# Hybrid decoder layer on one core: an own tile for a temporary of the early FFN products, two tiles for the third weight block of the joint FFN, and the final scalings spread over later passes

## The chip, the core and the metric

The kernel runs on one core of a Trainium2 chip. Five engines work side by side, each through its own list of instructions in order: PE (TensorE) multiplies matrices into PSUM, DVE (VectorE) and ACT (ScalarE) do elementwise work, POOL (GpSimd) does some elementwise work and issues transfers, SP (SyncE) issues most transfers between DRAM and SBUF. An instruction waits on semaphores that other engines or landed transfers raise; what stands behind it on its engine waits too.

The metric is the device time of one execution in microseconds (us).

## The reference

One layer: RWKV-7 time mixing and an indexer-selected sparse attention side by side, merged by gates, then a dense SwiGLU FFN and a last RMSNorm. 1024 tokens, width 1024, all in float32. The change touches the end of the merge, the FFN and the last norm:

```python
z = rmsnorm(h, norm2_g)                   # h: the layer's sum after the merge
g, u = split(z @ w_ffn_in, 2)             # D_FF = 2816
h = h + (silu(g) * u) @ w_ffn_out
out = rmsnorm(h, normf_g)
```

This is the core of it, written out in short.

## The kernel before

**Number format.** Every float32 operand x is split into a high part (ACT, L116) and the rest (DVE, L117: `lo = x - hi`), and a product is three matmuls for each 128 rows: hi·hi, hi·lo, lo·hi (`mm3`, L146, L147, L151). A matmul is 128 x 128 times 128 x 512.

**Tiling.** Everything stands transposed: 128 channels on the partitions, tokens along the row. The tokens are two halves of 512 (`HT`). The FFN's inner width is 22 blocks of 128 (`NFF`). Blocks 0 to 7 (`EARLY`) are done for each half apart; blocks 8 to 21 are done for both halves jointly in four groups (`JOINT`: 4, 3, 3 and 4 blocks), each followed by its part of the output product.

**Buffers.** Results of products go to PSUM: `acc` (three banks) and `mix` (five). `tmp()` gives the next of four [128, 512] tiles in SBUF; whoever takes one waits until its last user, often a store to DRAM, is done. Raw weights land in `wst` (three tiles), their parts in `whi`/`wlo` (two each).

**Order.** PE's list is written out by hand: generators yield counts of matmuls, and `fill`, `pump` and `tiles` slip FFN products of half 0 between the attention's products of half 1. The lists of the other engines follow from the order in which the program issues their instructions, with those under `high_priority` moved ahead.

**Early products.** While the attention of half 1 runs, `ahead(j, zs)` (L1327) computes for j = 8 to 21 two products p and x of half 0 with half a weight tile each, scales them by a row (L1335, L1337), adds them (L1338), forms silu(x) in t (`silu`, L1317 on ACT, L1318 on DVE) and stores p and t to `d_p[j]` (L1336, L1340). p, x and t are three `tmp()`. Just before it, `ffn_out` for half 0 adds blocks 0 to 7 to the sum in `d_h`: load into a `tmp()`, add (L1362), store (L1363).

**Merge and sums.** `merge(1, ...)` (L1183) multiplies the gates into the outputs of half 1 (L1199, L1213), with `mid` for the first half of the sum. `combined` (L1446) loads the stored z of half 0 (`d_z`, L1461), scales it into one of two `t` tiles (L1462) and builds the sums t1, t2 and t4 of both halves' activations.

**Joint tile.** For one block j, `joint_in` (L1505) needs five sums of products in place of six: two with `wb` (acc and mix, L1527 and L1530), the third with the first half of `wc` (L1533), the fourth with `wd` (L1535), and the fifth with the second half of `wc`, added in PSUM to the third (L1538). So the fifth may start only when L1533 has read the third. `sums` (L1480) forms the weight combinations on POOL (four operations, L1444); `blocks` (L1492) splits them into `wb`, `wc`, `wd`. Both are issued one tile ahead. In the groups, tiles 8, 9, 10, 12, 13, 15, 16, 18, 19, 20 prepare the next one's blocks; the first of a group gets its blocks from the output product of the group before.

**End.** `finish_out` (L1393) does the output product of the last group in three passes: half 0, the first 256 tokens of half 1, and the last 256. In each it adds eight products to h (L1425) and sums the squares (`Rms.add`, L259 on ACT, L260 on DVE). `norm_out` (L1383) then scales the eight rows (L1390) and stores them; it runs in the middle of the next pass, all eight rows at once.

Of the kernel before, what the change touches and what calls it, by code (L numbers as in the profile page):

```python
# [50 lines left out]
def block_kernel(ctx: ExitStack, tc: tile.TileContext, ins: dict, outT: bass.AP, stop=None, dbg=None):  # L51
# [1131 lines left out]
    def merge(half, zp, zs, jp=None):  # L1183
# [7 lines left out]
        if half:  # L1191
            mid = jp.tile([128, 8, HT], F32, tag="t3", name="mid")
            for d in range(8):
                w = weights(ins["w_o"][d][:, 0:4, :], 4)
                ga = tmp()
                SY.dma_start(ga, d_g[half][d])
                pa = acc()
                yield from mm3(pa, w, yt, nk=4)
                V.scalar_tensor_tensor(mid[:, d, :], ga, 1.0, pa, op0=ALU.add, op1=ALU.mult)  # L1199
# [5 lines left out]
        for d in range(8):  # L1205
            if half:
# [5 lines left out]
                ga = mid[:, d, :]  # L1212
# [113 lines left out]

    def ahead(j, zs):  # L1327
# [6 lines left out]
        p, x, t = tmp(), tmp(), tmp()  # L1334
# [7 lines left out]
    def ffn_out(f, g0, gn, halves, ring=None, raw=None, last=None):  # L1342
# [16 lines left out]
        def add(d, half, ps):  # L1359
            t = tmp() if ring is None else ring[:, (2 * d + half) % 8, :]  # L1360
# [22 lines left out]
    def norm_out(half, sq):  # L1383
# [4 lines left out]
        for k in range(8):  # L1388
            u = sq.h[:, k, sq.tok]
            V.scalar_tensor_tensor(u, u, par[:, P_NF + k:P_NF + k + 1], rb, op0=ALU.mult, op1=ALU.mult)  # L1390
            SY.dma_start(outT[k * 128:(k + 1) * 128, half * HT + sq.tok.start:half * HT + sq.tok.stop], u)

    def finish_out(zps, jp, f, g0, gn):  # L1393

        whi, wlo = (zps[0].tile([128, 8, gn, 128], F32R, tag=t, name=n) for t, n in (("s1", "fhi"), ("s3", "flo")))
        hs = [jp.tile([128, 8, HT], F32, tag="t3", name="h"), zps[1].tile([128, 8, HT], F32, tag="s1", name="h")]
        ws, before = [], None
        for half in range(2):
            for d in range(8):
                G.dma_start(hs[half][:, d, :], d_h[half][d])  # L1400
# [7 lines left out]
        for half, tok in ((0, slice(0, HT)), (1, slice(0, 256)), (1, slice(256, HT))):  # L1408
# [8 lines left out]
            for d in range(8):  # L1417
# [7 lines left out]
                V.tensor_tensor(h[:, d, tok], h[:, d, tok], ps, op=ALU.add)  # L1425
# [79 lines left out]
    def joint_in(f, gn, i, j, bs, ring, jp):  # L1505

        wb, wc, wd = prepared.pop(j)
        p1, t0, w, c = (ring[:, j % 2, e, :] for e in range(4))
        SY.dma_start(ring[:, j % 2, 0:2, :], d_p[j])
# [22 lines left out]
        with urgent():  # L1532
            V.tensor_tensor(c, w, pc, op=ALU.add)  # L1533
# [106 lines left out]
    if fill:  # L1640
        tiles(1)
    sb.close()
    (sz1, zp1), z1 = opened("right", "zp1"), []
    with tc.tile_pool(name="jp", bufs=1, side="right", reuse_waits="tile") as jp:
        run_over(merge(1, zp1, z1, jp))
# [15 lines left out]
        more = jp.tile([128, 8, HT], F32, tag="t3", name="more")  # L1661
        ring = zp1.tile([128, 2, 4, HT], F32, tag="s0", name="ring")
# [5 lines left out]
        finish_out(both, jp, f, *JOINT[-1])  # L1668
# [81 lines left out]
```

## Time and profile before

| What | us |
|---|---|
| Median of 3 runs (1744.35 to 1752.37) | 1746.75 |
| Profiled execution | 1742.06 |
| Its span | 1740.3 |
| PE busy | 1681.8 |
| DVE busy | 1178.5 |
| ACT busy | 823.6 |
| POOL busy | 177.2 |
| Span without PE's busy time (worked out) | 58.5 |

A row of a timeline gives start, duration, engine, line, operation, what it writes and reads, and in brackets how long the engine had been idle and what released it. "DVE tmp L1335" is the DVE instruction of line 1335 that writes `tmp`. A q behind an engine's name is its queue, which issues transfers. The idle time of PE stands in a few places: the start, the early products, the attention's softmax, the merge, the joint tiles and the last passes.

### The profile page before, as it was taken

What the parts mean: (1) busy time and instruction counts of PE and PEld (TensorE: products, weight loads), DVE (VectorE), ACT (ScalarE), POOL (GpSimd) and SP (SyncE); (2) the same over time, 40 slices, a digit from 0 to 9 for tenths busy, and PEclk for the clock granted to TensorE, in tenths of its full rate; (3) what the DMA queues carried; (4) which work ended last, traced back from release to release, by engine and by line L of the source; (5) the groups of instructions that cost most, each with busy time, mean ns of one, the idle gap of its engine ahead of it and who ended that gap; (6) DMA issues with size and microseconds to landing.
All of it is one profiled execution on the core that took longest, in us unless ns stands there. A gap on an engine that the chain in (4) does not pass through costs nothing.

```text
span 1740.3 us, 26809 instructions
## 1 busy us (share of the span) xinstructions
PE 1681.8 (97%) x9952; PEld 1382.1 (79%) x9952; DVE 1178.5 (68%) x2277; ACT 823.6 (47%) x1585; POOL 177.2 (10%) x179
## 2 busy tenths in 40 slices
PE   8999999999999999999999899999999999999997
PEld 6888888788877777877787688878788878787777
DVE  6789989857578457956885465674874463746566
ACT  6365998553444688645324266533442231322231
POOL 0000000010021111000100221000000321221320
PEclk9999999999999999999999899999999999999998
DMA  5542224536265524664342774476445446475532
GB/s 211 164 145 95 100 98 146 163 102 176 89 192 172 161 89 155 203 192 148 103 131 95 226 205 132 154 235 198 145 129 186 139 134 223 138 229 185 170 108 97
DMA packets 149090, 268.13 MB, mean 154 GB/s; under 512 B 38704, under 2 KB 63984, under 8 KB 148832
## 3 DMA queue, kind: packets, MB, share of 16 engines
q1 hardware_dynamic: 125600, 192.59, 34.5%
q10 hardware_dynamic: 15552, 47.75, 8.7%
q0 software_dynamic: 7808, 26.09, 5.5%
q8 instruction: 78, 1.28, 0.3%
q14 instruction: 52, 0.43, 0.1%
HBM read 195.54 MB, written 70.83 MB: 153 GB/s over the span
## 4 chain that ended last, share of the span: by engine, by line
PE 61%; DVE 9%; DMA 4%; ACT 3%; issue 2%; POOL 2%; SPq 0%; POOLq 0%; DVEq 0%; ACTq 0%
PE acc L146 14%; PE acc L151 13%; PE acc L147 13%; DVE wlo L117 2%; PE mix L1093 2%; PE mix L1518 2%; PE acc L161 2%; PE mix L1069 2%; PE mix L1522 2%; PE mix L1520 2%; PE mix L1083 2%; DMA wst<-in_w_ffn_in 1%; DMA d_h<-tmp 1%; PE mix L828 1%; PE mix L840 1%
## 5 line engine op out<-in xcount | busy, mean ns | idle before, releaser
L117 DVE TENSOR_TENSOR wlo<-wst,whi 128x1024 fp32r<-128x1024 f32 (+1 forms) x177 | 210.1, 1189 | 159.2 <-ACT whi L116 89.6
L116 ACT ACTIVATE whi<-wst 128x1024 fp32r<-128x1024 f32 (+1 forms) x177 | 173.9, 984 | 221.3 <-PE acc L147 147.9
L146 PE MATMUL acc<-zhi,whi 128*128 128x512 f32 x336 | 133.7, 398 | 7.8 <-DVE tmp L1335 7.4
L146 PE MATMUL acc<-u1hi,whi 128*128 128x512 f32 x352 | 140.3, 398 | 0.0
L147 PE MATMUL acc<-u1lo,whi 128*128 128x512 f32 x352 | 138.1, 392 | 0.0
L146 PE MATMUL acc<-u0hi,whi 128*128 128x512 f32 (+1 forms) x352 | 135.3, 387 | 1.8 <-DVE tmp L352 1.8
L147 PE MATMUL acc<-u0lo,whi 128*128 128x512 f32 (+1 forms) x352 | 133.8, 383 | 0.0
L147 PE MATMUL acc<-zlo,whi 128*128 128x512 f32 x336 | 132.1, 393 | 0.0
L146 PE MATMUL acc<-fhi,whi 128*128 128x512 f32 x236 | 92.8, 393 | 1.0 <-ACT whi L116 1.0
L147 PE MATMUL acc<-flo,whi 128*128 128x512 f32 x236 | 92.1, 390 | 1.0 <-DVE flo L117 1.0
L151 PE MATMUL acc<-u1hi,wlo 128*128 128x512 f32 x352 | 90.4, 396 | 0.0
L151 PE MATMUL acc<-zhi,wlo 128*128 128x512 f32 x336 | 87.2, 395 | 0.0
L151 PE MATMUL acc<-u0hi,wlo 128*128 128x512 f32 (+1 forms) x352 | 86.6, 385 | 0.0
L146 PEld LDWEIGHTS acc<-zhi,whi 128*128 128x128 f32 x336 | 63.7, 190 | 22.2 <-DVE tmp L1335 7.8
L146 PEld LDWEIGHTS acc<-u1hi,whi 128*128 128x128 f32 x352 | 67.1, 191 | 14.7 <-DVE tmp L343 0.4
L146 PEld LDWEIGHTS acc<-u0hi,whi 128*128 128x128 f32 x352 | 66.2, 188 | 15.2 <-ACT stg L116 2.2
L147 PEld LDWEIGHTS acc<-u1lo,whi 128*128 128x128 f32 x352 | 66.8, 190 | 13.3
L151 PEld LDWEIGHTS acc<-u1hi,wlo 128*128 128x128 f32 x352 | 65.7, 189 | 14.4 <-issue 1.2
L147 PEld LDWEIGHTS acc<-u0lo,whi 128*128 128x128 f32 x352 | 66.2, 188 | 12.2
L151 PEld LDWEIGHTS acc<-u0hi,wlo 128*128 128x128 f32 x352 | 64.0, 188 | 13.1 <-issue 0.7
L147 PEld LDWEIGHTS acc<-zlo,whi 128*128 128x128 f32 x336 | 63.7, 190 | 12.5
L151 PEld LDWEIGHTS acc<-zhi,wlo 128*128 128x128 f32 x336 | 62.9, 189 | 13.2 <-issue 0.3
(421 smaller groups left out, 3945.3 us busy)
## 6 DMA issues: line engine op xcount, KB each, us to landing
wst<-in_w_ffn_in SPq DMA_DIRECT2D x58, 512.0 KB, 3.6
wst<-in_w_in ACTq DMA_DIRECT2D x36, 512.0 KB, 3.4
wst<-in_w_in SPq DMA_DIRECT2D x27, 512.0 KB, 3.5
k<-d_k POOLq DMA_DIRECT2D x24, 512.0 KB, 7.5
more<-d_h SPq DMA_DIRECT2D x48, 256.0 KB, 4.3
d_h<-more SPq DMA_DIRECT2D x48, 256.0 KB, 3.8
h<-in_xT SPq DMA_DIRECT2D x32, 256.0 KB, 5.0
d_g<-tmp ACTq DMA_DIRECT2D x32, 256.0 KB, 2.5
```

The costliest lines, as they stand in the source:

```text
L116: A.activation(hi, x, AF.Copy)
L117: V.tensor_tensor(lo, x, hi.bitcast(F32), op=ALU.subtract)
L146: T.matmul(ps, whi[:, wk + k, :], ahi[:, ak + k, tok], start=k == 0, stop=False)
L147: T.matmul(ps, whi[:, wk + k, :], alo[:, ak + k, tok], start=False, stop=False)
L151: T.matmul(ps, wlo[:, wk + k, :], ahi[:, ak + k, tok], start=False, stop=k == nk - 1)
L161: T.matmul(ps, w[:, k, :], a[:, k, tok], start=k == 0 and w is whi and a is ahi, stop=k == nk - 1 and a is alo)
L1069: T.matmul(ps[:, :w], q[bi // 2][:, e, bi % 2 * 128:bi % 2 * 128 + 128], k[:, i, e, c:c + w], start=i == 0, stop=i == 1)
L1083: T.transpose(ps[:, j * 128:(j + 1) * 128], L[:, (c + j) * 128:(c + j + 1) * 128], ident)
L1093: T.matmul(py[64 * e:64 * e + 64, bi * 128:(bi + 1) * 128], v[:, j, 64 * e:64 * e + 64], pts[e][j // 4][:, j % 4, :], start=j == b, stop=j ...
L1518: T.matmul(ps, w[0][:, o + k, :], bhi[:, k, :], start=first_ and k == 0, stop=False, skip_group_check=not first_)
L1520: T.matmul(ps, w[0][:, o + k, :], blo[:, k, :], start=False, stop=False, skip_group_check=not first_)
L1522: T.matmul(ps, w[1][:, o + k, :], bhi[:, k, :], start=False, stop=k == 3, skip_group_check=not first_)
```

## The change

Three edits, and what they bring along:

1. **`spare`.** In `ahead`, x gets a tile of its own in place of a `tmp()`: one buffer while the attention runs, and in the merge one of the two `t` buffers that `combined` uses too. p and t stay `tmp()`.
2. **Third weight block.** `wc` is one tile for both parts, and its two buffers alternate (tag "wc", and the room of half of `mid`). `blocks(j + 1)` is issued behind the third addition of tile j, no longer at the tile's start. The tile's sums w and c are `tmp()`, which makes the ring smaller; `mid` and `more` are cut in two.
3. **Rows of the end.** `norm_out` hands back control after each row, and the later pass calls it once for each d. Half 0's h is in the tiles of `more`.

```diff
-            mid = jp.tile([128, 8, HT], F32, tag="t3", name="mid")
+            mid = [jp.tile([128, 4, HT], F32, tag=f"m{i}", name="mid") for i in range(2)]
...
+    spare = [tmp]
...
-        p, x, t = tmp(), tmp(), tmp()
+        p, x, t = tmp(), spare[0](), tmp()
...
             V.scalar_tensor_tensor(u, u, par[:, P_NF + k:P_NF + k + 1], rb, op0=ALU.mult, op1=ALU.mult)
             SY.dma_start(outT[k * 128:(k + 1) * 128, half * HT + sq.tok.start:half * HT + sq.tok.stop], u)
+            yield 0
...
-                if before is not None and d in (1, 3):
-                    next(before, None)
-                    if d == 3:
-                        run(before)
-            before = norm_out(half, sq)
-            next(before)
-        run(before)
+                if len(late) > 1:
+                    next(late[0], None)
+                if late and (d == 1 or d > 2):
+                    next(late[-1], None)
+            if len(late) > 1:
+                run(late.pop(0))
+            late.append(norm_out(half, sq))
+            next(late[-1])
+        for before in late:
+            run(before)
...
-            wc = [jp.tile([128, 8, 128], F32R, tag=t, name=t) for t in ("wchi", "wclo")]
+            wc = jp.tile([128, 2, 8, 128], F32R, tag="m1" if j % 2 else "wc", name="wc")
+            wc = [wc[:, 0], wc[:, 1]]
...
-        p1, t0, w, c = (ring[:, j % 2, e, :] for e in range(4))
+        p1, t0 = (ring[:, 2 * (j % 2) + e, :] for e in range(2))
+        w, c = tmp(), tmp()
...
-            if i + 1 < gn:
-                blocks(j + 1, jp)
...
-            V.tensor_tensor(c, w, pc, op=ALU.add)
+            third = V.tensor_tensor(c, w, pc, op=ALU.add)
+        if i + 1 < gn:
+            with tc.issue_after(third.ins):
+                blocks(j + 1, jp)
...
     with tc.tile_pool(name="at1", bufs=1, side="right", reuse_waits="tile") as ap:
+        spare[0] = lambda: ap.tile([128, HT], F32, tag="spare", name="spare")
...
+        spare[0] = lambda: jp.tile([128, HT], F32, tag="t", name="t", bufs=2)
...
-        more = jp.tile([128, 8, HT], F32, tag="t3", name="more")
-        ring = zp1.tile([128, 2, 4, HT], F32, tag="s0", name="ring")
+        ring = zp1.tile([128, 8, HT], F32, tag="s0", name="ring")
+        more = jp.tile([128, 4, HT], F32, tag="m0", name="more")
+        more = [more[:, i, :] for i in range(4)] + [ring[:, i, :] for i in range(4, 8)]
```

PE's list is the same in both kernels but for the names of the tiles. The other engines' lists change in three places that matter here. Line numbers behind the edits grow by 1 to 11 in the changed kernel (L1335 is L1338 there, L1533 is L1541, L1390 is L1393, L1425 is L1430).

First, the early products on DVE, blocks 8 to 10, where the attention of half 1 begins. The order stays; the waits don't. DMAHW1 is the landing of the d_h store that the profile shows issued at 976.70 us, DMAHW6 that of the one at 971.83 us, DMAHW2 that of block 8's p. Before:

```order
L1335 TENSOR_TENSOR tmp<-acc,row 128x512 [waits DMAHW1_49,PE_49]
L1318 SCALAR_TENSOR_TENSOR tmp<-tmp 128x512 [waits DMAHW6_49,Activation_49]
L1337 TENSOR_TENSOR tmp<-acc,row 128x512 [waits DMAHW2_49,PE_49]
L117 TENSOR_TENSOR wlo<-wst,whi 128x1024 [waits DMAHW5_49,Activation_49]
L1338 TENSOR_TENSOR tmp<-tmp 128x512 [waits DVE_49]
L1335 TENSOR_TENSOR tmp<-acc,row 128x512 [waits DMAHW5_49,PE_49]
L1318 SCALAR_TENSOR_TENSOR tmp<-tmp 128x512 [waits Activation_49]
```

And changed:

```order
L1338 TENSOR_TENSOR tmp<-acc,row 128x512 [waits DMAHW6_49,PE_49]
L1319 SCALAR_TENSOR_TENSOR tmp<-tmp,spare 128x512 [waits DMAHW4_49,Activation_49]
L1340 TENSOR_TENSOR spare<-acc,row 128x512 [waits DVE_49,PE_49]
L117 TENSOR_TENSOR wlo<-wst,whi 128x1024 [waits DMAHW5_49,Activation_49]
L1341 TENSOR_TENSOR spare<-spare,tmp 128x512 [waits DVE_49]
L1338 TENSOR_TENSOR tmp<-acc,row 128x512 [waits DMAHW2_49,PE_49]
L1319 SCALAR_TENSOR_TENSOR tmp<-tmp,spare 128x512 [waits DMAHW1_49,Activation_49]
```

The wait for DMAHW1 has moved from block 9's p to its t, five instructions later; x (L1340) waits for no transfer.

Second, one joint tile on DVE, from the first addition (L1527) to the fourth (L1535), in the last group. Before, the next tile's weights stand ahead of the second and third additions:

```order
L1527 TENSOR_TENSOR ring<-ring,acc 128x512
L117 TENSOR_TENSOR wlo<-wst,whi 128x512
L117 TENSOR_TENSOR wlo<-s_14946,whi 128x512
L1539 SCALAR_TENSOR_TENSOR ring<-ring 128x512
L1530 TENSOR_TENSOR ring<-ring,mix 128x512
L117 TENSOR_TENSOR flo<-ring,fhi 128x512
L1533 TENSOR_TENSOR ring<-ring,mix 128x512
L117 TENSOR_TENSOR wdlo<-wst,wdhi 128x512
L1535 TENSOR_TENSOR ring<-ring,mix 128x512
```

Changed (the names are the same, `wc` holds both parts of the third block):

```order
L1535 TENSOR_TENSOR ring<-ring,acc 128x512
L117 TENSOR_TENSOR flo<-ring,fhi 128x512
L1538 TENSOR_TENSOR tmp<-ring,mix 128x512
L1541 TENSOR_TENSOR tmp<-tmp,mix 128x512
L117 TENSOR_TENSOR wlo<-wst,whi 128x512
L117 TENSOR_TENSOR wlo<-s_14959,whi 128x512
L117 TENSOR_TENSOR wc<-wst,wc 128x1024
L117 TENSOR_TENSOR wdlo<-wst,wdhi 128x512
L1546 TENSOR_TENSOR tmp<-tmp,mix 128x512
```

The four subtractions of the weights have moved behind the third addition (L1541). The subtraction `flo<-ring,fhi`, which belongs to the tile before, stands ahead of it in both; its high part `fhi` stands on ACT behind that of `wst` in both.

Third, the second pass of the end on DVE. Before, all eight scalings of half 0 stand in a row:

```order
L1425 TENSOR_TENSOR h<-h,acc 128x256
L260 TENSOR_TENSOR sacc<-sacc,tmp 128x256
L1390 SCALAR_TENSOR_TENSOR h<-h,par,mix 128x512 x8
L1425 TENSOR_TENSOR h<-h,acc 128x256 x3
L260 TENSOR_TENSOR sacc<-sacc,tmp 128x256 x2
```

Changed:

```order
L1430 TENSOR_TENSOR h<-h,acc 128x256
L261 TENSOR_TENSOR sacc<-sacc,tmp 128x256
L1393 SCALAR_TENSOR_TENSOR more<-more,par,mix 128x512 x2
L1430 TENSOR_TENSOR h<-h,acc 128x256
L1393 SCALAR_TENSOR_TENSOR more<-more,par,mix 128x512
L261 TENSOR_TENSOR sacc<-sacc,tmp 128x256
L1430 TENSOR_TENSOR h<-h,acc 128x256
L1393 SCALAR_TENSOR_TENSOR more<-more,par,mix 128x512
L261 TENSOR_TENSOR sacc<-sacc,tmp 128x256
```

Two scalings stand together, then one for each addition. In the merge, one more effect of the `t` buffers: the first two scalings of `d_z` (L1462), which stood between the merge's first gate products, now stand with the other six behind it, and their loads with them.

More of the change, by code (lines that the diff above doesn't have):

```diff
@@ L245, in __init__ @@
         def __init__(self, h, tok=slice(0, HT)):
-            self.h, self.tok, self.n = h, tok, (tok.stop - tok.start) // 128
+            self.h = h if callable(h) else lambda k: h[:, k, :]
+            self.tok, self.n = tok, (tok.stop - tok.start) // 128
             self.acc = tp.tile([128, HT], F32, tag="sacc", name="sacc", bufs=2)
@@ L1198, in merge @@
                 yield from mm3(pa, w, yt, nk=4)
-                V.scalar_tensor_tensor(mid[:, d, :], ga, 1.0, pa, op0=ALU.add, op1=ALU.mult)
+                V.scalar_tensor_tensor(mid[d // 4][:, d % 4, :], ga, 1.0, pa, op0=ALU.add, op1=ALU.mult)
         for j in range(4, 8):
@@ L1211, in merge @@
                 yield from mm3(pb, w, yt, nk=4, ak=4)
-                ga = mid[:, d, :]
+                ga = mid[d // 4][:, d % 4, :]
                 V.scalar_tensor_tensor(gb, gb, 1.0, pb, op0=ALU.add, op1=ALU.mult)
@@ L1359, in add @@
         def add(d, half, ps):
-            t = tmp() if ring is None else ring[:, (2 * d + half) % 8, :]
+            t = tmp() if ring is None else ring[(2 * d + half) % 8]
             SY.dma_start(t, d_h[half][d])
@@ L1388, in norm_out, with finish_out @@
         for k in range(8):
-            u = sq.h[:, k, sq.tok]
+            u = sq.h(k)[:, sq.tok]
             V.scalar_tensor_tensor(u, u, par[:, P_NF + k:P_NF + k + 1], rb, op0=ALU.mult, op1=ALU.mult)
             SY.dma_start(outT[k * 128:(k + 1) * 128, half * HT + sq.tok.start:half * HT + sq.tok.stop], u)
-    def finish_out(zps, jp, f, g0, gn):
+            yield 0
+    def finish_out(zps, more, f, g0, gn):
         whi, wlo = (zps[0].tile([128, 8, gn, 128], F32R, tag=t, name=n) for t, n in (("s1", "fhi"), ("s3", "flo")))
-        hs = [jp.tile([128, 8, HT], F32, tag="t3", name="h"), zps[1].tile([128, 8, HT], F32, tag="s1", name="h")]
-        ws, before = [], None
+        h1 = zps[1].tile([128, 8, HT], F32, tag="s1", name="h")
+        hs = [lambda k: more[k], lambda k: h1[:, k, :]]
+        ws, late = [], []
         for half in range(2):
             for d in range(8):
-                G.dma_start(hs[half][:, d, :], d_h[half][d])
+                G.dma_start(hs[half](d), d_h[half][d])
         def w(d):
@@ L1507, in joint_in @@
         wb, wc, wd = prepared.pop(j)
-        p1, t0, w, c = (ring[:, j % 2, e, :] for e in range(4))
-        SY.dma_start(ring[:, j % 2, 0:2, :], d_p[j])
+        p1, t0 = (ring[:, 2 * (j % 2) + e, :] for e in range(2))
+        w, c = tmp(), tmp()
+        SY.dma_start(ring[:, 2 * (j % 2):2 * (j % 2) + 2, :], d_p[j])
         if j + 1 < NFF:
             sums(j + 1, jp)
-            if i + 1 < gn:
-                blocks(j + 1, jp)
         def mm(ps, w, o, b, first_=True):
@@ L1639, in block_kernel @@
             pump(abs(n))
-    if fill:
-        tiles(1)
+        if fill:
+            tiles(1)
     sb.close()
@@ L1667, in block_kernel @@
                 run(*ffn_out(f, g0, gn, [0, 1], more, jp, lambda: blocks(g0 + gn, jp)))
-        finish_out(both, jp, f, *JOINT[-1])
+        finish_out(both, more, f, *JOINT[-1])
     sz1.close()
```

8 lines of the change are left out of this document (4 added, 4 removed).

## The prediction

> **What bounds the kernel now.** I read the page's busy times first, then the waits of PE, and then the timelines of PE and of the engine that each large wait names. All times are microseconds from the span's start.
>
> ```profile
> PE 1681.8 (97%) x9952; PEld 1382.1 (79%) x9952; DVE 1178.5 (68%) x2277; ACT 823.6 (47%) x1585; POOL 177.2 (10%) x179
> ...
> PE acc L146 <- DVE tmp L1335: 7.4, 1, 7.4
> PE mix L1518 <- DVE ring L1533: 7.2, 6, 2.7
> PE acc L146 <- DVE mid L1199: 2.7, 1, 2.7
> PE acc L146 <- DVE h L1425: 1.9, 1, 1.9
> ```
>
> The first row is the busy time of each engine; the others are what PE waited for, with total, number of times and longest. PE is busy for 1681.8 of 1740.3, so it is the bound, and the order and number of its matmuls are the same in both kernels. Only PE's idle time can go, 58.5 in all, and the change touches four causes that hold 7.4 + 7.2 + 2.7 + 1.9 = 19.2 of it. I look for the end of each wait in its own stretch. The change is thus worth about 1% at most before anything is lost, and half of that is about what a measurement of this kernel can tell from no change (0.5% is 8.7 us).
>
> **1. The own tile of the early products.** The rows are those of PE, DVE, ACT and SP's queue, and the window (sum, PE, PEld, DVE, ACT, POOL, then the granted clock, the DMA share and GB/s).
>
> ```profile
> 995.74 0.79 PE L146 MATMUL acc<-zhi,whi 128*128 128x512 f32 x1 [7.39 <-DVE tmp L1335]
> 1000.92 0.39 PE L146 MATMUL acc<-zhi,whi 128*128 128x512 f32 x1
> 1006.46 0.77 PE L1083 MATMUL mix<-kc,L 128*128 128x128 f32 x5 [0.75 <-ACT L L1074]
> ...
> 995.00 0.69 DVE L1335 TENSOR_TENSOR tmp<-acc,row 128x512 f32<-128x512 f32 x1 [12.34 <-DMA d_h<-tmp]
> 1003.46 0.48 DVE L1071 CUSTOM_DVE_ANT_0 L<-mix,bias 128x320 f32<-128x320 f32 x1
> ...
> 985.16 0.63 ACT L1317 ACTIVATE tmp<-tmp 128x512 f32<-128x512 f32 x1 [4.78 <-DMA d_h<-tmp]
> ...
> 971.83 0.32 SPq L1363 DMA_DIRECT2D d_h<-tmp  x1
> 976.70 0.32 SPq L1363 DMA_DIRECT2D d_h<-tmp  x1
> 978.23 0.32 SPq L1336 DMA_DIRECT2D d_p<-tmp  x1
> ...
> 987.00:1007.00 20.00, 11.86 (x48) 9.34 (x47) 10.46 (x21) 3.24 (x5) 0.70 (x2) 0.74 0.67 241
> ```
>
> PE stops at 988.35 (995.74 - 7.39) because all three `acc` buffers are full, and DVE cannot empty one: p of block 9 takes the `tmp` whose store to d_h, issued at 976.70, lands only at 995.0. The granted clock in this window is 0.74, and the first twelve matmuls after the stop take 5.18 (995.74 to 1000.92) where twelve take 2.72 (rows of part 4). So the stop costs 7.39, then 2.46 of slow clock, then 0.75 for the softmax that DVE reaches late: 10.6.
>
> In the changed order p of block 9 takes the buffer whose store was issued at 971.83; that one landed by 985.16, where ACT's tanh was released by it. x has its own tile. PE then finds free buffers and runs the 7.5 of work that it has up to L1083 (1006.46 - 988.35 - 10.6) by 995.9. But the late store does not go away: t of block 9 now takes that buffer, and p of block 10 the one whose store was issued at 978.23. DVE runs in order, so the softmax (L1071) still stands behind 995.0: tanh 0.63, then t, x, one weight subtraction and one addition (three at 0.60 apart, the subtraction at 1.13), 3.6 in all, so L1071 comes at about 998.6 instead of 1003.46, and L1083 at 1001.6 instead of 1006.46. That is 4.9 earlier. PE has then been idle for 5.7, and I take the slow restart of 2.46 again, since 5.7 is nearer to 7.39, after which it was seen, than to the 2.74 of part 2, after which it wasn't. **Gain 2.4**; bounds 0 (the store lands later still) and 10.0 (no second stop).
>
> [...]
>
> **2. The d_z scalings leave the merge.** PE, DVE and SP's queue:
>
> ```profile
> 1135.12 0.47 PE L146 MATMUL acc<-yhi,whi 128*128 128x512 f32 x1 [2.74 <-DVE mid L1199]
> 1137.93 0.39 PE L146 MATMUL acc<-yhi,whi 128*128 128x512 f32 x1
> ...
> 1133.03 0.75 DVE L1462 SCALAR_TENSOR_TENSOR t<-t,par,row 128x512 f32<-128x512 f32 x1 [1.96 <-DMA t<-d_z]
> 1134.30 0.68 DVE L1199 SCALAR_TENSOR_TENSOR mid<-tmp,acc 128x512 f32<-128x512 f32 x1
> ...
> 1128.45 0.32 SPq L1461 DMA_DIRECT2D t<-d_z  x1
> ```
>
> The first two d_z tiles use the two `t` buffers, which blocks 17 to 21 of `ahead` now occupy. So the load at 1128.45 (landed 1133.03, 4.6 later) is gone here, and the first gate load takes its place in SP's queue: it lands at about 1133.0, L1199 runs at once, and PE starts at 1133.85 instead of 1135.12. **Gain 1.3**; bounds 0 and 2.7. Twelve matmuls took 2.81 after this stop: no slow clock.
>
> **3. They land in a full stretch.** Windows, then DVE and PE, and what the eight L1462 waited for in all:
>
> ```profile
> 1240.00:1260.00 20.00, 20.00 (x90) 16.55 (x89) 19.67 (x30) 9.15 (x13) 0.00 (x0) 1.00 0.41 132
> ...
> 1270.53 0.75 DVE L1462 SCALAR_TENSOR_TENSOR t<-t,par,row 128x512 f32<-128x512 f32 x1 [0.90 <-DMA t<-d_z]
> 1271.20 1.22 DVE L117 TENSOR_TENSOR wlo<-wst,whi 128x1024 fp32r<-128x1024 f32 x1
> ...
> 1273.42 1.98 PE L151 MATMUL acc<-zhi,wlo 128*128 128x512 f32 x8
> ...
>   DMA t<-d_z: 2.9, 2
> ```
>
> DVE is busy for 19.67 of 20 and PE for all 20. The lower half of a weight is ready at 1272.42 and PE uses it at 1273.42: 1.0 of room. Two more scalings of 0.75 come in, and their two loads now wait too, for 0 to 4.6 together. 1.5 + 0.2 of waiting - 1.0 = **loss 0.7**; bounds 0 and 5.1.
>
> **4. The third weight block.** One joint tile is five products of twelve matmuls; the fifth adds to the sum of the third, so it waits for the third addition, L1533.
>
> ```profile
> 1633.55 0.39 PE L1518 MATMUL acc<-t,whi 128*128 128x512 f32 x1
> 1636.27 0.39 PE L1518 MATMUL mix<-t,whi 128*128 128x512 f32 x1
> 1647.27 0.50 PE L1518 MATMUL mix<-t,wchi 128*128 128x512 f32 x1 [2.69 <-DVE ring L1533]
> ...
> 1631.81 4.18 SPq L127 DMA_DIRECT2D wst<-in_w_ffn_in  x2
> 1647.85 0.33 SPq L127 DMA_DIRECT2D wst<-in_w_ffn_in  x1
> ...
> 1638.09 1.28 POOL L1444 TENSOR_TENSOR s<-wst 128x512 f32<-128x512 f32 x1 [6.33 <-DMA wst<-in_w_ffn_in]
> 1640.82 1.29 POOL L1444 TENSOR_TENSOR wst<-s,wst 128x512 f32<-128x512 f32 x1
> 1652.61 1.29 POOL L1444 TENSOR_TENSOR s<-wst 128x512 f32<-128x512 f32 x1 [9.13 <-DMA wst<-in_w_ffn_in]
> ...
> 1642.14 0.63 ACT L116 ACTIVATE whi<-wst 128x512 fp32r<-128x512 f32 x1 [2.10 <-POOL wst L1444]
> ...
> 1642.80 1.23 DVE L117 TENSOR_TENSOR wlo<-wst,whi 128x512 fp32r<-128x512 f32 x1 [5.37 <-ACT whi L116]
> 1646.54 0.68 DVE L1533 TENSOR_TENSOR ring<-ring,mix 128x512 f32<-128x512 f32 x1
> ```
>
> A product takes 2.72, so counted from a tile's first matmul the third ends at 8.2, the fourth at 10.9, the tile at 13.6. Before, DVE's subtraction for the next tile's weights (1642.80) stands ahead of L1533 and waits for ACT, which waits for POOL's third sum (ends 1642.11), which waits for a load of 6.3 (1631.81 to 1638.09). L1533 ends 5.1 behind POOL's third sum. In the changed order the subtractions stand behind L1533, and so do those of the third block, which now has two tiles and needn't wait for PE.
>
> The tie to POOL is not cut, though. ACT still has the high part of the previous tile's f (fhi) behind that of the weights (whi), and DVE has the low part of that f ahead of L1533: third sum + 0.63 + 0.63 + 0.68 + 0.60 + 0.69 = 3.2 behind instead of 5.1. The load that starts the sums waits for the subtraction of the third block, three subtractions after L1533, at 11.4 of the tile ahead; with L for its time, the third sum ends at L + 1.8, L1533 at L + 5.1, and PE stalls above L = 5.8. Once a tile is late, the next one waits L - 3.9. Of the six waits, five then vanish or nearly so; in the last group L was 6.3 and then 4.8 (1647.85 to 1652.61), which leaves about 0.4 + 0.9. **Gain 7.2 - 1.3 = 5.9**; bounds 7.2 (no tie) and 0.6 (all six loads as slow as 6.3: four waits of 0.45 and two of 2.4 stay).
>
> The two sums that now take `tmp` use three of four buffers for each tile, each free again within a tile: nothing.
>
> **5. The rows at the end.** DVE and PE:
>
> ```profile
> 1709.12 5.35 DVE L1390 SCALAR_TENSOR_TENSOR h<-h,par,mix 128x512 f32<-128x512 f32 x8
> 1733.26 3.22 DVE L1390 SCALAR_TENSOR_TENSOR h<-h,par,mix 128x256 f32<-128x256 f32 x8 [2.16 <-PE mix L283]
> ...
> 1714.85 0.39 PE L146 MATMUL acc<-fhi 128*128 128x256 f32 x1 [1.87 <-DVE h L1425]
> ```
>
> Eight scalings in a row hold DVE for 5.35, and PE runs out of `acc` buffers for 1.87. One for each d, 0.67 each, fits beside the additions. The last eight (1733.26) and what follows stay as they are. **Gain 1.9**; bounds 1.0 and 2.3 (the bursts of the third pass cost PE nothing, so nothing is won there).
>
> **Sum.** 2.4 + 1.3 - 0.7 + 5.9 + 1.9 = 10.8. The profiled execution took 1742.06 (1.8 of it around the span) and would take 1731.3, a ratio of 0.9938. The median of the runs, 1746.75, lies 4.7 above it; the same ratio gives **1735.9**.
>
> **Rivals.**
> - *The stall is only moved (A).* The own tile does not do what it says, because t and p of the next blocks take the same late buffers: the 995.0 landing moves behind the extra traffic and term 1 is 0. For it: t9 and p10 do wait for those stores. Against it: the buffer that p9 takes was stored ten earlier, so two `acc` buffers do come free. Gain 8.4, 1738.3.
> - *The wait for L1533 stays, by way of fhi (B).* Every load of the six is as slow as the slowest: term 4 is 0.6, gain 5.5, 1741.2. For it: in the row of 1638.09 POOL waits for the load; against it: the next took 4.8.
> - *The stop in part 1 goes altogether (D).* t and p of blocks 9 and 10 land in time: 10.0 there, gain 18.4, 1728.3. Against it: the two stores were issued 18 before 995.0 and nothing in the change speeds them.
> - *Slower: DVE waits for d_z in the full stretch (C).* All eight loads wait as the one at 1133.03 did, 1.96, since `t` has two buffers and no load is done ahead: 1.5 + 8 x 1.96 - 1.0 = 16.2 instead of 0.7, so 4.7 slower than before, 1751.5. It decides from 1.4 for each load (the other terms give 11.5). Against it: of the six that stand there before, one waited, 0.90.
>
> **Chances.** The forecast 0.58, A 0.17, B 0.11, D 0.07, C 0.07. The forecast and D are faster by over 0.5%; but the forecast clears that bound by 2 us only, so I move 0.05 of it to "same": faster 0.60, same 0.33 (A, B and that part), slower 0.07. The range holds all but C and the worst corner of B: the bounds summed reach 1724 and 1750, and 1726 to 1747 leaves out some 2 in 10.
>
> **What would show it.** Term 1: PE's stop at 988 gone and another of 5 to 6 just ahead of L1083 near 996, with a granted clock well under 1 behind it; no second stop would mean D. Term 2: the wait for `mid` at 1135 down to 1.5. Term 3: L1470 with waits on d_z after 1240, and small new idle of PE there. Term 4: `mix` waiting for the third addition in one or two tiles, with ACT's fhi right behind POOL's third sum. Term 5: no wait for L1430 in the second pass. The prediction is wrong if a store of the 976 to 978 pair lands much later than 995, or if a joint tile's load takes over 7.

## The result, and the profile after

| | before | changed |
|---|---|---|
| Median of 4 runs each, us | 1745.55 (1744.25 to 1752.37) | 1729.32 (1726.89 to 1732.12) |
| Profiled execution | 1742.06 | 1726.89 |
| Its span | 1740.3 | 1725.1 |

The ratio is 0.990, with a 95% interval of 0.9869 to 0.993: the changed kernel is faster by 0.7 to 1.3%. The forecast was 1735.9, in a range of 1726 to 1747. The sign was that of the forecast, and so were most of the mechanisms; the gain was larger: 15.2 between the two spans and 16.2 between the medians, where the sum said 10.8.

The page's busy times of the changed kernel, and what PE waited for there at the places of the change (total, times, longest):

```profile
PE 1681.5 (97%) x9952; PEld 1383.4 (80%) x9952; DVE 1178.9 (68%) x2277; ACT 825.0 (48%) x1585; POOL 182.1 (11%) x179
...
PE mix L1070 <- DVE mx L1072: 3.9, 4, 2.7
PE mix L1526 <- DVE tmp L1541: 1.1, 3, 0.4
```

PE's work is the same to 0.3. Its waits for p (7.4), for `mid` (2.7) and for the rows of h (1.9) are gone from the list, the wait for the third addition has fallen from 7.2 to 1.1, and one wait has grown, that of L1070 for the softmax on DVE.

Since PE's list of 9952 matmuls is the same in both, one can set the start of each matmul of one execution beside the start of the same matmul in the other. The differences, summed by stretch (cut at 979, 1021, 1118, 1140, 1229, 1252, 1367, 1696 and 1732 of before), say where the time went, for each run of this study, against the profiled execution of before (minus: shorter):

| kernel | up to 979 | early products | merge | norm | full stretch | joint | end |
|---|---|---|---|---|---|---|---|
| changed | +1.2 | -4.7 | -1.6 | +1.6 | 0.0 | -9.4 | -2.2 |
| changed again (e4) | +2.4 | -4.7 | -0.5 | 0.0 | 0.0 | -9.6 | -2.2 |
| own tile alone (e1) | +2.1 | -5.1 | -1.1 | +1.6 | 0.0 | -0.2 | +1.5 |
| joint alone (e2) | +0.3 | -1.0 | -0.2 | 0.0 | 0.0 | -9.3 | 0.0 |
| end alone (e3) | +1.7 | -1.7 | +1.5 | 0.0 | 0.0 | -0.4 | -2.2 |
| blocks split early (e5) | +1.1 | -4.4 | -1.3 | +1.6 | 0.0 | +23.8 | -2.2 |
| one tile, late (e6) | -0.7 | -4.2 | -0.2 | 0.0 | 0.0 | -3.9 | -2.2 |
| fhi first (e7) | +5.9 | -3.1 | -1.5 | 0.0 | 0.0 | -10.4 | -2.2 |
| stores not waited for (e8) | +0.7 | -10.5 | -1.7 | +1.6 | 0.0 | -9.3 | -2.2 |
| ACT's queue (e9) | +0.5 | -4.8 | -0.2 | 0.0 | 0.0 | -8.9 | -2.2 |
| both (e10) | -1.3 | -8.6 | -0.8 | +1.6 | 0.0 | -10.7 | -2.2 |
| p and sums on ACT's queue (e11) | +4.2 | -6.2 | -0.8 | 0.0 | 0.0 | -10.7 | -2.2 |
| both again (e12) | +1.6 | -6.3 | -1.3 | +1.6 | 0.0 | -10.7 | -2.2 |

The table also shows what one execution is worth. The first column, where no kernel differs from another, varies by 7. The early products took 1.0 to 1.7 less in the two runs that have the old code there (e2, e3), so before's own profile was a little unlucky at that place: PE's stop was 7.39 in it, 6.32 and 6.64 in them, and the granted clock from 988 to 1008 was 0.74 in it, 0.83 in them. In the joint stretch before has a stop of 0.38 of its own (1684.93, PE L161 waiting for ACT's fhi), which with its restart makes 0.5 to 1.0 of that column in every other run but e6, whatever its code. Of three entries that fit no edit, the +1.5 in e3's merge and the +1.6 of the norm are stretches of slow clock (last section); the +1.5 in e1's end is taken for one too, by its size.

**Early products.** PE, DVE, ACT and SP's queue of the changed kernel, and the window of the prediction:

```profile
996.48 0.51 PE L1070 MATMUL mix<-k,q 128*128 128x384 f32 x2
999.65 1.01 PE L1070 MATMUL mix<-k,q 128*128 128x384 f32 x2 [2.66 <-DVE mx L1072]
1002.05 1.33 PE L1084 MATMUL mix<-kc,L 128*128 128x128 f32 x5 [1.40 <-ACT L L1075]
...
985.48 0.69 DVE L1338 TENSOR_TENSOR tmp<-acc,row 128x512 f32<-128x512 f32 x1 [1.17 <-DMA d_h<-tmp]
995.36 0.69 DVE L1338 TENSOR_TENSOR tmp<-acc,row 128x512 f32<-128x512 f32 x1 [5.61 <-DMA d_p<-tmp]
999.10 0.48 DVE L1072 CUSTOM_DVE_ANT_0 L<-mix,bias 128x320 f32<-128x320 f32 x1
...
994.26 0.63 ACT L1318 ACTIVATE tmp<-spare 128x512 f32<-128x512 f32 x1 [6.73 <-DMA d_h<-tmp]
...
978.36 0.32 SPq L1366 DMA_DIRECT2D d_h<-tmp  x1
...
987.00:1007.00 20.00, 15.95 (x70) 12.98 (x69) 11.31 (x26) 7.03 (x14) 3.64 (x8) 0.83 0.78 276
```

The stop has moved as the prediction described: p of block 9 passes at 985.5, t of block 9 (on ACT) waits for the same store until 994.3 and p of block 10 for block 8's p until 995.4, and the softmax on DVE comes 3.7 later. PE now stops in two pieces, 2.66 and 1.40, and two matmuls that took 0.51 ahead of the first stop take 1.01 behind it: the clock fell again, to 0.83 in this window.

**The full stretch.** Rows of DVE's scalings of d_z in the changed kernel (duration in ns, least, median, most; then an empty list of waits), the loads' issue on SP, and the next work of DVE that had to wait:

```profile
L1470 DVE SCALAR_TENSOR_TENSOR t<-t,par,row x8: 744/746/753, 1240.7 to 1279.9; 128x512 f32<-128x512 f32 x8
...
its engine sat idle before it (us, times) until:
who waited for it (us, times):
...
1232.67 0.42 SPq L1469 DMA_DIRECT2D t<-d_z  x1
1238.23 0.38 SPq L1469 DMA_DIRECT2D t<-d_z  x1
...
1244.44 1.22 DVE L117 TENSOR_TENSOR wlo<-wst,whi 128x1024 fp32r<-128x1024 f32 x1 [1.71 <-ACT whi L116]
...
1257.00:1277.00 20.00, 20.00 (x90) 16.57 (x89) 19.34 (x29) 9.38 (x14) 0.00 (x0) 1.00 0.47 153
```

All eight stand here now, and none waited for its load: the first two loads are issued 8.0 and 2.5 ahead of the first scaling. A little behind these DVE still stands idle for 1.71, and PE is busy for all 20 of the window.

**The joint tile**, the second of the last group (SP, POOL, ACT, DVE):

```profile
1623.64 0.90 SPq L127 DMA_DIRECT2D wst<-in_w_ffn_in  x2
...
1631.36 1.29 POOL L1452 TENSOR_TENSOR wst<-s,wst 128x512 f32<-128x512 f32 x1
...
1632.68 0.63 ACT L116 ACTIVATE whi<-wst 128x512 fp32r<-128x512 f32 x1 [0.31 <-POOL wst L1452]
1633.22 0.62 ACT L116 ACTIVATE fhi<-ring 128x512 fp32r<-128x512 f32 x1
...
1633.87 0.71 DVE L117 TENSOR_TENSOR flo<-ring,fhi 128x512 fp32r<-128x512 f32 x1 [4.48 <-ACT fhi L116]
1635.28 0.69 DVE L1541 TENSOR_TENSOR tmp<-tmp,mix 128x512 f32<-128x512 f32 x1
1635.88 0.69 DVE L117 TENSOR_TENSOR wlo<-wst,whi 128x512 fp32r<-128x512 f32 x1
```

This is the tie of the prediction, row by row: POOL's third sum ends at 1632.65, the weights' high part follows, then fhi, then flo on DVE, which had stood idle for 4.48, then the third addition, which ends 3.3 behind the sum (3.2 was worked out). The weights' low part comes behind it.

**The end.** DVE in the second pass:

```profile
1696.65 1.40 DVE L1393 SCALAR_TENSOR_TENSOR more<-more,par,mix 128x512 f32<-128x512 f32 x2
1697.97 0.41 DVE L1430 TENSOR_TENSOR h<-h,acc 128x256 f32<-128x256 f32 x1
1698.30 0.74 DVE L1393 SCALAR_TENSOR_TENSOR more<-more,par,mix 128x512 f32<-128x512 f32 x1
```

The additions stand 1.3 apart with one scaling between them, and PE no longer waits for L1430.

### The profile page after: what moved, and what is told of

It reads as the page before. It is cut to its first block, busy times and chain, and to the rows that moved or that the text cites. A ratio compares the mean times of both kernels' runs of the same rounds, so it can differ in the third digit from the quotient of the medians.

```text
span 1725.1 us, 26801 instructions
## 1 busy us (share of the span) xinstructions
PE 1681.5 (97%) x9952; PEld 1383.4 (80%) x9952; DVE 1178.9 (68%) x2277; ACT 825.0 (48%) x1585; POOL 182.1 (11%) x179
## 4 chain that ended last, share of the span: by engine, by line
PE 75%; DVE 11%; ACT 6%; issue 3%; DMA 3%; POOL 1%; SPq 0%; DVEq 0%; POOLq 0%; ACTq 0%
PE acc L146 15%; PE acc L147 15%; PE acc L151 15%; PE mix L1526 3%; PE mix L1530 3%; PE mix L1528 3%; PE acc L161 2%; PE mix L1094 2%; PE mix L1070 2%; DVE wlo L117 2%; PE mix L1084 2%; ACT junk L985 2%; ACT junkl L985 1%; PE mix L935 1%; DVE junk L982 1%
## 5 line engine op out<-in xcount | busy, mean ns | idle before, releaser
L117 DVE TENSOR_TENSOR wlo<-wst,whi 128x1024 fp32r<-128x1024 f32 (+1 forms) x177 | 202.1, 1143 | 127.3 <-ACT whi L116 56.8
L146 PEld LDWEIGHTS acc<-u0hi,whi 128*128 128x128 f32 x352 | 66.2, 188 | 15.2 <-ACT stg L116 2.1
```

The lines of the kernel that those rows point to most:

```text
L117: V.tensor_tensor(lo, x, hi.bitcast(F32), op=ALU.subtract)
L146: T.matmul(ps, whi[:, wk + k, :], ahi[:, ak + k, tok], start=k == 0, stop=False)
```

## The experiments

### The three parts alone, and the whole again

The first three take one part of the change's diff each, on the kernel before: e1 the lines with `spare`, e2 those on `wc`, `w`, `c`, `mid`, `more`, `ring` and `blocks`, e3 those on `late` and `yield 0`. The fourth is the changed kernel once more, on the same chip.

> The kernel before with the own tile of the early products alone. Theory (the gains are made in separate places and add up): the stop of 7.4 us at 988 goes, a shorter one of about 4 us in all comes near 997, and the merge's wait for mid goes: about 6 us faster than before (4.7 in the early products, 1.5 in the merge, as the two traces show). Rival (the own tile only moves the stop): under 2 us.

> The kernel before with the change to the joint tiles alone. Theory: 8 to 9 us faster; PE's waits for the third addition fall from 7.2 us to about 1, each stop that goes also frees 0.2 to 0.3 us that its restart costs, and the two waits of 0.5 us for the low part of f go. Rival (only the idle time of the waits counts, the rest is chance of the profiled execution): 6 us.

> The kernel before with the spread of the final scalings alone. Theory: PE's wait of 1.9 us for L1425 goes, 2.0 to 2.5 us faster. Rival (DVE needs 1.45 us for each d beside PE's 1.44, so the last pass ends as late as before): no gain.

> The changed kernel once more, on the same chip as the three parts. Theory: 16 us faster than before, the sum of the three parts within 2 us. Rival (the parts overlap or need each other): the sum of the parts differs from the whole by 4 us or more.

| run | ratio to before | interval |
|---|---|---|
| e1, own tile alone | 0.9973 | 0.9957 to 0.9989 |
| e2, joint alone | 0.9943 | 0.9921 to 0.9965 |
| e3, end alone | 0.9973 | 0.9957 to 0.9989 |
| e4, whole | 0.9898 | 0.9877 to 0.9919 |

The parts give 4.7 + 10.0 + 4.7 = 19.4 of 1746.17, the whole 17.8, with intervals of about plus or minus 3 to 4 on each: within these they add up, and each is a gain of its own. The stretches of the table say the same more sharply: but for the slow clock, each part's gain stands in its own column and nowhere else. The end is 2.2 shorter in every run that has the edit (the 4.7 of e3's median has an interval of 1.9 to 7.5); the joint stretch 9.3 alone and 9.6 in the whole. The time of e2, 6.1 to 13.8 with its interval, doesn't rule out the rival's 6; its trace does.

### Which part of the joint change makes the gain

Two kernels take half of it each, on the changed kernel. e5 splits the next blocks at the tile's start again, with two tiles for the third block; e6 keeps the split behind the third addition, with one tile.

```diff
 e5
         if j + 1 < NFF:
             sums(j + 1, jp)
+            if i + 1 < gn:
+                blocks(j + 1, jp)
...
-        if i + 1 < gn:
-            with tc.issue_after(third.ins):
-                blocks(j + 1, jp)
 e6
-            wc = jp.tile([128, 2, 8, 128], F32R, tag="m1" if j % 2 else "wc", name="wc")
+            wc = jp.tile([128, 2, 8, 128], F32R, tag="wc", name="wc")
```

> The changed kernel with two tiles for the third weight block, but with the next blocks split at the tile's start, as before. Theory (the order on DVE makes the gain): the subtraction that waits for POOL stands ahead of the third addition again, and PE's waits for that addition come back to 4 to 7 us; 4 to 7 us slower than the changed kernel. Rival (the second tile makes the gain): waits of about 1 us, as fast as the changed kernel.

> The changed kernel with the next blocks split behind the third addition, but with a single tile for the third weight block. Theory (order alone is not enough): the third block can be written only when PE has ended the tile, so the raw tile comes free 3 to 4 us later, and with it the next load and POOL's sums; PE's waits for the third addition are 4 us or more, 3 to 8 us slower than the changed kernel. Rival (order is all): waits of about 1 us, as fast.

e5: ratio 1.0094 (1.0076 to 1.0112), 16 slower than before, not 10 faster. PE's waits, and PE and DVE at one of the six stops:

```profile
PE mix L1528 <- DVE tmp L1543: 23.4, 6, 5.3
...
1651.92 0.80 PE L1528 MATMUL mix<-t,wc 128*128 128x512 f32 x1 [5.29 <-DVE tmp L1543]
...
1650.07 1.19 DVE L117 TENSOR_TENSOR wlo<-s,whi 128x512 fp32r<-128x512 f32 x1 [5.21 <-ACT whi L116]
```

The direction was right. The waits are three to six times the expected 4 to 7, and the loss is larger still: against the changed kernel the joint stretch is 33 longer, of which the waits are 22; slow matmuls behind the long stops are most of the rest (the granted clock was 0.66 from 1650 to 1660, behind the stop shown). DVE's order shows where the waits come from. In the tile of block 18 of before and of e5 (the sums of the weights carry numbers; in e5 14856 is block 19 and 14959 block 20, in before 14844 and 14946):

```
before                                   e5
wlo<-s_14844                             wlo<-s_14856
L1527 first addition                     L1537 first addition
L1530 second addition                    L1540 second addition
L1533 third addition                     wlo<-s_14959
                                         L1543 third addition
```

In e5 a split of block 20 stands in the tile of block 18, ahead of its third addition, and there it waits for POOL's sum of weights whose load was issued only at 1643.54. Before, with one tile, no split of block 20 stands there. That the second tile is what gave the scheduler the room is the likely reading; it was not tried apart, since e5 and before also differ in where w and c lie. What is shown: with two tiles and no hold the waits are 23.4 where before had 7.2, and with the hold behind the third addition they are 1.1.

e6: ratio 0.9912 (0.9894 to 0.993), not to be told from the changed kernel by its time. The expectation of 4 us of waits for the third addition fell: one wait of 0.4 is left. I had the raw tile come free later, and the load and the sums with it; whatever they did, the third addition was in time. So the order alone removes these waits. What the second tile adds stands elsewhere, 5.4 in the joint column, most of it in one stop at the end of the last tile. PE there:

```profile
1674.44 0.50 PE L161 MATMUL acc<-fhi 128*128 128x512 f32 x1 [1.87 <-ACT fhi L116]
...
1677.14 0.63 PE L161 MATMUL acc<-flo,fhi 128*128 128x512 f32 x1
```

It waits for the last block's f. The steps to it stand on DVE, in both kernels, behind the split of a weight of the output product, and that weight's load held ACT until 1670.44 here (2.03 of waiting for it), about 2 later in the tile than in the changed kernel (1668.21). Behind the stop the clock is slow (0.63 for one matmul at 1677.14, 0.39 at 1675.73). In medians these 5.4 don't show, so they come from one profile only.

### What is left of the wait for the third addition

```diff
+        with urgent():
-        V.tensor_tensor(p1, p1, pc, op=ALU.add)
-        V.scalar_tensor_tensor(t0, t0, 0.5, p1, op0=ALU.mult, op1=ALU.mult)
-        split(f[0][:, i, :], f[1][:, i, :], t0)
+            V.tensor_tensor(p1, p1, pc, op=ALU.add)
+            V.scalar_tensor_tensor(t0, t0, 0.5, p1, op0=ALU.mult, op1=ALU.mult)
+            split(f[0][:, i, :], f[1][:, i, :], t0)
```

> The changed kernel with the last three steps of a joint tile moved ahead, so that on ACT the high part of the previous f stands ahead of that of the weights that wait for POOL's third sum. Theory (what is left of the wait for the third addition comes by way of this order): the three waits of 1.1 us in all vanish with the 0.25 us that each restart costs, DVE's stop of 3 to 4.5 us ahead of that f in two tiles of the last group goes; 1 to 2 us faster than the changed kernel. Rival (it comes from the load alone): no change.

Ratio 0.9909 (0.9894 to 0.9925): no difference that the time can show. In the profile the step is there: fhi now stands ahead of the weights on ACT, the three waits of 1.1 have become one of 0.4, and the joint stretch is 1.0 shorter.

```profile
1634.27 0.62 ACT L116 ACTIVATE fhi<-ring 128x512 fp32r<-128x512 f32 x1
1636.81 0.63 ACT L116 ACTIVATE whi<-wst 128x512 fp32r<-128x512 f32 x1 [1.92 <-POOL wst L1452]
```

So the tie by way of fhi is shown. In the changed kernel, where the wait had already fallen to 1.1, it was worth 1.0.

### What holds the early products

e8 takes the waits for six stores away: the last two of half 0's sums and those of blocks 8 and 9 send a row tile's bytes in place of the temporaries', so the results of these blocks are not the layer's.

```diff
-            SY.dma_start(d_h[half][d], t)
+            SY.dma_start(d_h[half][d], z0[2] if halves == [0] and d >= 6 else t)
...
-        SY.dma_start(d_p[j][:, 0, :], p)
+        SY.dma_start(d_p[j][:, 0, :], row if j < 10 else p)
...
-        SY.dma_start(d_p[j][:, 1, :], t)
+        SY.dma_start(d_p[j][:, 1, :], row if j < 10 else t)
```

> The changed kernel in which the last two stores of half 0 to d_h and the four stores of blocks 8 and 9 to d_p take their bytes from a row tile that stays, so the same bytes move but no temporary waits for them (these results are not the layer's). Theory (the stores' landing at 994 to 995 is all that holds the early products): the stop ahead of L1070 and L1084 near 997 goes, 4 to 5 us faster than the changed kernel. Rival (the attention's loads of k and q, or ACT's softmax, are late by themselves): under 1.5 us.

```profile
997.21 0.77 PE L1084 MATMUL mix<-kc,L 128*128 128x128 f32 x5 [0.76 <-ACT L L1075]
...
985.00:1005.00 20.00, 19.24 (x101) 16.05 (x99) 13.97 (x35) 11.44 (x22) 6.05 (x12) 1.00 0.90 276
...
L1339 SPq DMA_DIRECT2D d_p<-row x2: 332/390/448, 823.6 to 824.7; - x2
...
968.47 0.92 SPq L1366 DMA_DIRECT2D d_h<-row  x2
```

Of the stop 0.76 is left, the clock stays at 1.00, and the stretch is 10.5 shorter than before's, 5.8 more than with the change. So the loads of k and q, which stay where they were, are not what held it. But the run does more than take the waits away. A row tile is ready early, so these stores are also issued early: those to d_p at 824, those to d_h at 968.5, where the changed kernel issues its last one to d_h at 978.36. All six thus leave the stretch in which k, v and q are loaded. What of the 5.8 is the waits, and what is the room that the other transfers gain, e8 can't say; the next runs bear on it. In time it is 0.989 (0.9873 to 0.9906): against the changed kernel's 0.990 the expected 4 to 5 us don't show.

e9 leaves the results alone and moves these six stores to ACT's queue; e10 and e12 add e7's order to it; e11 is e10 with t of blocks 8 and 9 back on SP.

```diff
-            SY.dma_start(d_h[half][d], t)
+            (A if halves == [0] and d >= 6 else SY).dma_start(d_h[half][d], t)
...
-        SY.dma_start(d_p[j][:, 0, :], p)
+        (A if j < 10 else SY).dma_start(d_p[j][:, 0, :], p)
...
-        SY.dma_start(d_p[j][:, 1, :], t)
+        (A if j < 10 else SY).dma_start(d_p[j][:, 1, :], t)
```

> The changed kernel in which the last two stores of half 0 to d_h and the four stores of blocks 8 and 9 to d_p are issued by ACT, on its queue, not by SP behind SP's weight loads. Theory (a store waits for what stands ahead of it in its own queue, the loads of k, v and q being in another): the stores land within 10 us, the stop near 997 goes as in the run without the waits, 4 to 6 us faster than the changed kernel. Rival (the transfer engines are full from 970 to 993 whichever queue a store is in): they land at 990 or later, under 2 us.

> The stores on ACT's queue and the earlier high part of f together, on the changed kernel. Theory: the two add up, 6 to 8 us faster than the changed kernel, a ratio to before near 0.986. If the stores do not land sooner: 1 to 3 us faster, 0.989.

> As the run with both, but with t of blocks 8 and 9 stored by SP again, so that ACT never waits for DVE's t before it splits the next weights. Theory (what is left of the stop near 995 is the landing of the next weight tile, since the transfers are full until 993): within 2 us of the run with both. Rival (ACT's issue of t's store is what holds the weights): 2 to 4 us faster than it.

> The run with both once more. Theory: a ratio to before of 0.987 again, 4 to 7 us faster than the changed kernel. If the first one was chance: 0.990, no better than the changed kernel.

| run | ratio to before | interval |
|---|---|---|
| e9, six stores on ACT's queue | 0.9915 | 0.9902 to 0.9929 |
| e10, and fhi first | 0.9871 | 0.9854 to 0.9888 |
| e12, the same again | 0.9878 | 0.9856 to 0.9899 |
| e11, t back on SP | 0.9895 | 0.9881 to 0.9909 |

The last store to d_h landed sooner on ACT's queue, in 8.0 against 15.8 on SP's. The transfers between 965 and 1000, the changed kernel first, then e9 (number of issues, KB each, and us to landing, which the view has for one of them in each):

```profile
d_h<-tmp SPq DMA_DIRECT2D x3, 256.0 KB, 15.8
```

```profile
d_h<-tmp ACTq DMA_DIRECT2D x2, 256.0 KB, 8.0
```

So for this store the first half of e9's theory held. The one before it held DVE's p of block 9 until 983.88 in e9, 11.25 behind its issue at 972.63, where the changed kernel shows 11.97 (973.51 to 985.48). The gain did not come (0.9915, where the changed kernel has 0.990). The stop does not go as in e8, because the next thing is late: the next weights, whose load stands in the same full stretch (from 970 to 993 the transfer engines' share is 0.97 in the changed kernel and 0.99 in e9). ACT of e10, then of e11:

```profile
991.16 1.06 ACT L116 ACTIVATE whi<-wst 128x1024 fp32r<-128x1024 f32 x1 [3.74 <-DMA wst<-in_w_ffn_in]
```

```profile
997.93 1.06 ACT L116 ACTIVATE whi<-wst 128x1024 fp32r<-128x1024 f32 x1 [4.55 <-DMA wst<-in_w_ffn_in]
```

In the table the early stretch is -4.8 in e9, as with the change, and -8.6, -6.2 and -6.3 in the others: somewhere between nothing and two thirds of the 5.8. Part of this spread is the clock: from 988 to 1008 it was 0.83 in e9, as in the changed kernel, 0.91 in e11 and e12, and 1.00 in e10, and e10 and e12 are the same kernel. e11's wait tells that ACT's issue of t's store is not what holds the weights; e11 is not faster than the runs with both, as that rival would have it. The runs with both are the fastest of this study, 1.2 to 1.3% under before, and 0.2 to 0.3% under the two timings of the changed kernel; their intervals overlap with those, so a gain on the changed kernel is likely but not shown.

## Why the prediction was right, and where its sizes were off

**Bound and accounting.** Right: PE's work is unchanged and only its idle time went.

**Term 1, own tile (2.4 forecast, 4.7 in the profile).** The mechanism was right to the instruction. The size was low on two counts. The store's landing took 15.9 here (978.36 to 994.26) and not 18.2, so PE stood for 4.1 and not 5.7; and the slow clock cost some 1.8 (of 10.6 lost before, 5.9 remain, less 4.1 of idle) and not 2.46. Against the two runs that have the old code (-1.0 and -1.7) the edit is worth 3 to 4, which is nearer to the forecast. Rival A (the stop is merely moved, nothing won) is out by e1, and D (the stop goes) didn't occur; in e8, where it does go, the stretch is 10.5 shorter, near the 10.0 forecast for that. The median measured, 1729.3, lies next to D's 1728.3, though D is not what happened: the total alone would not have told them apart.

The shortened stop paid for a slow restart again, as the sum had it. My reason for that, that 5.7 is nearer to 7.39 than to 2.74, did not hold: the clock fell here behind a stop of 2.66, and in the norm behind one of 0.77 (below); with the same code in the merge, e3 has slow matmuls behind a stop of 2.40, and e10 has none behind its two stops of 0.55 and 1.88 here. In these runs the length of a stop does not settle it, so that the 2.46 was rightly taken was in part luck.

**Term 2, merge (1.3 forecast, 1.6).** The cause was right; the size came out of two errors that cancel. ACT and PE of the changed kernel:

```profile
1119.26 0.63 ACT L116 ACTIVATE yhi<-ylo 128x512 fp32r<-128x512 f32 x1 [1.77 <-DMA ylo<-d_ya]
...
1130.49 0.47 PE L146 MATMUL acc<-yhi,whi 128*128 128x512 f32 x1
```

The wait for `mid` is gone altogether, where the sum let 1.5 of it stay: the first gate load, issued at 1126.31, was used by L1200 at 1129.66, 3.4 later and not 4.6. That is 2.65. But 1.06 is lost a little ahead, where PE now waits three times for a half of y (0.22 each, and the restarts), because y's first load lands late. Every run with the own tile loses 0.6 to 1.5 there, e2 and e3 at most 0.2. The column is thus between 0.2 and 1.7 in the other runs with the edit; in e4, the same kernel, 0.84 of the wait for `mid` stayed and the gain was 0.5.

**Term 3, full stretch (a loss of 0.7 forecast, 0.0).** Wrong in two steps. The two loads were to wait, for 0.2 in the sum and up to 4.6 in its bound; they are issued at 1232.67 and 1238.23, ahead of need, and cost nothing. And DVE's room was taken as the 1.0 at 1272, too little for the 1.5 of added scaling; but the two scalings stand at 1240.7, where DVE had more of it (1.71 of idle is still left at 1244.44). Rival C, which needed 1.4 of waiting for each load, found none.

**Term 4, joint tiles (5.9 forecast, 8.4 to 9.4).** The waits fell by 6.1 (7.2 to 1.1), where 5.9 was worked out, and what remains comes by way of fhi as described (e7). That the remainder was so well met is in part luck: it was to be 0.4 and 0.9 in the last group, which has none, and is 0.3, 0.4 and 0.4 in the three groups before it. The term that was mis-sized is the price of a stop. It is more than the wait in brackets, as these rows of before show: the last four matmuls ahead of a stop, the first behind it, and the next product.

```profile
1643.52 1.07 PE L1522 MATMUL mix<-zhi,wdlo 128*128 128x512 f32 x4
1647.27 0.50 PE L1518 MATMUL mix<-t,wchi 128*128 128x512 f32 x1 [2.69 <-DVE ring L1533]
1650.13 0.39 PE L1518 MATMUL acc<-t,whi 128*128 128x512 f32 x1
```

The matmul at 1647.27 was due at 1643.52 + 4 x 0.227 = 1644.43, 2.84 earlier, and the twelve behind it take 2.86 in place of 2.72: the stop costs 2.98, and the same matmul moved by 2.97 in the changed kernel. That is 0.3 on top, and it is so at all six stops of before for the third addition: the first matmul starts 0.15 to 0.16 later than the wait in brackets says, and the twelve take 2.85 to 2.86. The change removes three stops and most of three more, and with them two of 0.48 for the low part of f in the products between the groups, which I had left out:

```profile
1516.83 0.50 PE L147 MATMUL acc<-flo,whi 128*128 128x512 f32 x1 [0.48 <-DVE flo L117]
```

6.1 + 3 x 0.3 + 2 x (0.48 + 0.3) = 8.6, against 8.4 measured without the 1.0 of before's own stop at 1684.93. In e1 and e3, which have the old joint code, the clock also fell behind the long stop (last section), which cost them another 1.4; against them the edit is worth about 9. Rival B (six slow loads) did not occur.

**Term 5, end (1.9 forecast, 2.2).** The same 0.3: 1.87 + 0.3.

**Sum.** By the measured terms the change itself is worth 3.0 to 4.7, 0.2 to 1.6, nothing, 8.4 and 2.2, some 14 to 17. The forecast of 10.8 lay 3 to 6 under it: 2.8 by the price of stops and the two waits for the low part of f, 0.7 by a loss that did not come, and the rest by the early products, as far as before's one execution lets it be known.

## What to carry to other kernels

- When a store's source rotates through a small pool, count which later instruction gets each buffer next: an own tile for one of them only hands the wait on, and what that is worth is the work that now stands ahead of the wait. A run that takes these waits away (e8) gives a bound for the rest; look at when its transfers are issued before you put all of it down to the waits.
- Double-buffering a prepared operand without holding its preparation behind the urgent instruction can cost more than it brings: work whose input comes late may then stand ahead of the urgent one on the same engine (e5: 23.4 of waits in place of 7.2).
- Price a stop of PE by when the next matmul was due, not by the idle time that the profile names: here 0.3 on top of each of the six stops for the third addition.

## What was not expected of the hardware

**The clock fell behind the same short stops in some executions and not in others.** In the norm of half 1 PE waits 0.19 to 0.20 and then 0.77 to 0.78 in the timelines of before, the changed kernel, e4 and e9 to e12. By the table's column the matmuls behind it cost 1.6 more than before's in 6 of the 13 other profiles, with the same instructions; in the changed kernel the clock is 0.50 there for 3.3 (below). The changed kernel twice, PE and the window 1228 to 1241, first the first run, then e4:

```profile
1233.64 0.50 PE L1283 MATMUL acc<-zhi,whi 128*128 128x512 f32 x1 [0.77 <-ACT zhi L1265]
1233.97 2.75 PE L1283 MATMUL acc<-zhi,wlo 128*128 128x512 f32 x7
...
1228.00:1241.00 13.00, 11.99 (x42) 8.74 (x41) 13.00 (x21) 5.57 (x9) 0.00 (x0) 0.87 0.48 169
```

```profile
1235.42 0.50 PE L1283 MATMUL acc<-zhi,whi 128*128 128x512 f32 x1 [0.77 <-ACT zhi L1265]
1235.76 1.78 PE L1283 MATMUL acc<-zhi,wlo 128*128 128x512 f32 x7
...
1228.00:1241.00 13.00, 12.00 (x49) 8.92 (x48) 13.00 (x21) 6.91 (x11) 0.00 (x0) 1.00 0.44 159
```

Seven matmuls take 2.75 in one and 1.78 in the other. The same is seen behind longer stops. In the merge before has no slow matmul behind 2.74; e3, with the same code there, has them behind 2.40 (four take 1.91, where four take 1.07 at full clock). In the last group before has none behind 2.69; e1, with the same code, has them behind 2.75, and e3 behind 2.41. Rows of e3, then of e1:

```profile
1135.07 0.47 PE L146 MATMUL acc<-yhi,whi 128*128 128x512 f32 x1 [2.40 <-DVE mid L1199]
1137.60 1.91 PE L151 MATMUL acc<-yhi,wlo 128*128 128x512 f32 x4
```

```profile
1644.95 0.76 PE L1520 MATMUL mix<-t,wchi 128*128 128x512 f32 x1 [2.75 <-DVE ring L1535]
1645.51 0.63 PE L1522 MATMUL mix<-t,wchi 128*128 128x512 f32 x1
```

In before the granted clock is 0.50 from 990.6 to 1000.7, in and behind the stop of 7.39, and 1.00 from 988.4 to 990.5 and from 1000.8 to 1010.0. In the changed kernel it is 0.50 from 999.0 to 1005.7, at the end of the stop of 2.66 and behind it, and from 1234.5 to 1237.8, behind the 0.77; on both sides of these two it is 1.00. So a difference of 1.6 between two profiles at such a place says nothing of the code, and a stop that is removed may save this price too, in the executions that would have paid it (1.4 in e1 and e3, above).

**One store landed sooner on another queue.** While k, v and q are loaded, one and the same 256 KB store to d_h took 15.8 on SP's queue in the changed kernel and 8.0 on ACT's in e9. Whether SP's weight loads ahead of it make the difference was not tried apart. The transfer engines are full in both (0.97 and 0.99 from 970 to 993), and what the stores gain the next weight load, still on SP's queue, does not: by the landings that the traces record it took 14.7 in the changed kernel (977.76 to 992.47) and 17.9 in e9 (976.89 to 994.75).
